# Second mixer's seven-product gates: the third product's tiles split later, forms of x in fewer steps, the norm's bias added by accumulating DMAs

## The chip, the core and the metric

One core of one Trainium2 chip runs the whole program. The metric is the device time in microseconds (us). Five engines work side by side, each on its own queue in order: TensorE (PE, with PEld for its weight loads), VectorE (DVE), ScalarE (ACT), GpSimd (POOL) and SyncE (SP). SP and POOL mostly issue DMAs here. Engines wait for one another through semaphores.

## What is computed

A trunk of two layers on x of 512 positions by 1024 channels in float32. Each layer has a token mixer and a ConvFFN, both with a residual and a layer norm:

```python
for i in range(DEPTH):                      # DEPTH = 2
    y = gla_mixer(h, ...) if i == 0 else gdn_mixer(h, ...)
    h = layer_norm(ALPHA * h + y, ln_g[i, 0], ln_b[i, 0])
    h = layer_norm(ALPHA * h + conv_ffn(h, ffn_w_in[i], ffn_conv_w[i], ffn_w_out[i]), ln_g[i, 1], ln_b[i, 1])

def gdn_mixer(x, w_in, conv_w, a_log, dt_bias, norm_w, w_out):
    qkv, gate, beta_lin, a_lin = split(x @ w_in)     # gate: 1024 columns
    ...
    o = rms_norm(gdn_chunked(qc, kc, vc, beta, gc), norm_w)
    return (from_head_chunks(o) * silu(gate)) @ w_out
```

The change is in the second mixer, the gated DeltaNet (gdn): in its projection to `gate`, 512 x 1024 by 1024 x 1024, and in the layer norm's bias that is brought back for the residual behind it.

## The kernel before, in words

**Products in split parts.** A float32 matrix product is made of three products of high and low parts (wh·xh, wl·xh, wh·xl). `split_out` (L718) makes the parts of a tile: a cast on ACT (the high part) and a subtraction on DVE (the low part). A weight tile of 128 x 1024 thus costs a load, a cast and a split.

**The gate in seven products.** `gated` (L1255 on) makes the gate's 2 x 2 block product with seven products instead of eight, in the order of `GATED` (L33): b21, b11, t1, b22, t2, t3, t4. Each is 24 "fold" matmuls, and uses two weight tiles and one *form* of x. Of the weights only b21, b11 and b22 are split as they are loaded; the others are sums, which the memory side makes: `issue_gated` (L452 to L469) splits a tile and then has POOL issue an accumulating DMA (L465) that adds the next block of the weights to the same tile. So t1's tiles (called gw) are b11's tiles with b12 added, and each is there one DMA after b11's own split. The tiles of b22 (called raw) get b12 added in the same way.

**How far ahead tiles are split.** `prefetch` (L471) issues the splits of the next tiles of the plan, as far as `self.look` says: with 3, three tiles beyond those taken. `gated` sets 3 at its start, and 2 within t3, so t4 runs with 2 in both mixers that call it.

**The order.** The program is written as coroutines that a small scheduler (`spawn`, `pump`, a model clock) puts between the matmuls when the program is built. The order in which it reaches an instruction is the order in each engine's queue; nothing is reordered at run time. A number behind `yield` tells how long the model clock waits.

**What runs beside the gate products.** While PE does the folds, the recurrence of the gdn runs in the gaps. `inverses` makes triangular inverses, the V and R matmuls of 64 x 64, in turns; DVE copies their results to the tiles `rm` (L1863 for quarters, L1883 for halves), two heads at a time. `chain(g)` (L1935 on) then walks through the four chunks of heads 0 to 3 (g = 0) and of heads 4 to 7 (g = 1): ks, vn, kT, qs, s and o on PE; on ACT `vn` (L1960) and `kd` (L1967), scaled copies out of PSUM; on DVE `yy`, the state (L1980 for the first chunk, a copy; L1983 later) and `v` (L1989, L1991). vn reads rm of all four heads; s needs vn and kd; the state copy frees a PSUM tile for later use.

**Forms of x.** `x_forms_within` makes the forms w1, v4, v2 and v3 from quarters a, b, c, d of x. a and b are sums xh + xl on DVE (L1163). c and d come through DMAs (`whole`, L1218 to L1224): first a copy of xh into a tile xq, then an accumulating DMA of xl onto it, all from POOL's queue. `both` (L1176) makes sums and differences of them, and `put` splits the result back into xh and xl.

**The residual.** The residual h lies in HBM during the mixer. `unspill` (L971) brings its eight tiles back, multiplies each by the layer norm's gain row (L989) and adds its bias row (L990) on DVE; `out_proj` (L615) then adds the mixer's output.

Of the kernel before, what the change touches and what calls it, by code (L numbers as in the profile page):

```python
# [8 lines left out]
F32 = mybir.dt.float32  # L9
# [4 lines left out]
ALU = mybir.AluOpType  # L14

P = 128
D = 1024
S = 512
# [55 lines left out]
def blk(i, n=P):  # L74
    return slice(i * n, i * n + n)


class Trunk:
# [893 lines left out]
    def unspill(self, gb_rows):  # L972

        nc = self.nc
        self.h = [[None, None] for _ in range(NTB)]
        gb = [self.slot("gb") for _ in range(4)]
        for hf in range(2):
            for tb in range(NTB):
                t = self.resid("h")
                nc.gpsimd.dma_start(t, self.hd[blk(tb), blk(hf, S)])  # L980
                self.h[tb][hf] = t
            for i in range(2):
                nc.gpsimd.dma_start(gb[2 * i + hf], gb_rows[i][blk(hf, S)].partition_broadcast(P))

        def affine():
            for hf in range(2):
                for tb in range(NTB):
                    t = self.h[tb][hf]
                    nc.vector.tensor_mul(t, t, gb[hf])  # L989
                    nc.vector.tensor_add(t, t, gb[2 + hf])  # L990
                    self.set(("h", tb, hf))
                    yield 1.8

        self.spawn(affine(), 9.0)

# [212 lines left out]
    def x_forms_within(self, forms, part, pair, full, both):  # L1208


        nc = self.nc

        def put(name, ts, odd, tok):
            for k, t in enumerate(ts):
                self.split_out(part(self.xh, odd, tok, k), part(self.xl, odd, tok, k), pair(t))
            forms[name] = (odd, tok)
            self.set(("form", name), 2.0)

        def whole(odd, tok):
            ts = [self.slot("xq") for _ in range(2)]  # L1220
            for x, op in ((self.xh, ALU.bypass), (self.xl, ALU.add)):
                for k, t in enumerate(ts):
                    nc.gpsimd.dma_start(pair(t), part(x, odd, tok, k).bitcast(F32), accum_op=op)
            return ts  # L1224

        yield from self.until(("rm", 1))
        a = full(0, 256)
        yield 1.5
        b = full(1, 256)
        yield 1.5  # L1230
        both(a, b, ALU.subtract, b)
        yield 2.0
        put("w1", b, 0, 256)
        yield from self.until(("rm", 5))
        c = whole(0, 0)
        d = whole(1, 0)
        yield from self.until(("used", "a11"))
        yield 4.0
        both(c, a, ALU.subtract, a)
        yield 2.0  # L1240
        both(b, c, ALU.subtract, b)
        yield 2.0
        both(b, d, ALU.add, d)
        c = None
        yield 2.0
        put("v4", d, 1, 0)
        d = None
        yield 3.0
        put("v2", b, 0, 0)
        b = None  # L1250
        yield from self.until(("used", "w1"))
        yield 1.0
        put("v3", a, 0, 256)

    def gated(self, forms, tag, done, last):  # L1255


        nc = self.nc
        acc = [[self.psum("fold") for _ in range(2)] for _ in range(2)]
        top, high, right = ([None, None] for _ in range(3))  # L1260

        def operand(form, c, r):
            if isinstance(forms.get(form), tuple):
                odd, tok = forms[form]
                chunk, tok = 2 * c + odd, tok + r * P
                return self.xh[:, chunk, tok:tok + P], self.xl[:, chunk, tok:tok + P]
            if form in forms:
                cols = slice(c % 2 * 256 + r * P, c % 2 * 256 + r * P + P)
                return tuple(t[:, cols] for t in forms[form][c // 2])
            chunk = 2 * c + (form != "a11")  # L1270
            tok = r * P + (256 if form == "a22" else 0)
            return self.xh[:, chunk, tok:tok + P], self.xl[:, chunk, tok:tok + P]

        def copied(ps):
            t = self.slot(tag)
            nc.scalar.copy(t, ps)
            return t

        def update(name, r):
            p, x = acc[0][r], acc[1][r]  # L1280
            if name == "b21":
                top[r] = copied(x)
            elif name == "b11":
                nc.vector.tensor_add(top[r], top[r], p)
                done(r, 1, top[r], top[r])
            elif name == "t1":
                high[r] = copied(x)
            elif name == "b22":
                right[r] = copied(x)
            elif name == "t2":  # L1290
                nc.vector.tensor_sub(right[r], right[r], p)
                done(r, 0, right[r], right[r])
            elif name == "t3":
                self.third = nc.vector.tensor_sub(high[r], high[r], p)
                self.after = None, self.third
                done(2 + r, 0, high[r], high[r])
            elif name == "t4":
                done(2 + r, 1, self.slot(tag), p)

        self.look = 3  # L1300
        for name, form, at in GATED:
            if form[0] in "vw":
                self.wait(("form", form))
            def terms(i, w, r):
                for j in range(2):
                    begin = name in ("b11", "b21", "t1") and i + j == 0
                    self.tm_terms(acc[at][r], *operand(form, i + j, r), *w[j], begin, i + j == 3, True)
                if i:
                    update(name, r)

            if name in ("t1", "t2", "t3"):
                w = [self.weight() for _ in range(2)]
                for r in range(2):
                    for i in (0, 2):
                        if name == "t3" and r and i:
                            self.look = 2
                        terms(i, w[i // 2], r)
                        if name != "t3" or not r:
                            self.pump()
                        if r:  # L1320
                            self.spend()
            else:
                for i in (0, 2):
                    w = self.weight()
                    if name == "t4":
                        self.after = ()
                    for r in range(2):
                        terms(i, w, r)
                        self.pump()
                    self.spend()  # L1330
            self.set(("used", form))
            if last:
                forms.pop(form, None)
        self.look = LOOKAHEAD
# [299 lines left out]
    def gdn(self, li, g, b):  # L1634
        nc = self.nc
# [11 lines left out]
        q, k, v, am, rm, pj = ([None] * DH for _ in range(6))  # L1647
# [284 lines left out]
        sg = [[None, None] for _ in range(NTB)]  # L1932
# [111 lines left out]
                self.spawn(finish(hf, half))  # L2044
        forms = {"apart": False}
        self.spawn(self.x_forms(forms))
        self.gated(forms, "sg", gate_done, True)
        self.wait(("r2", 1))
        self.unspill(spilled)
        self.mixer_out(y, li, g, b)  # L2050
# [76 lines left out]
```

## Time and profile before

| what | value |
|---|---|
| three runs | 1225.78, 1225.42, 1224.86 us; median 1225.42 us |
| the profiled execution | 1226.22 us, of which the span from first to last instruction is 1224.4 us |
| mean granted clock of TensorE | 0.997 |
| TensorE busy | 1212.0 us, 99% |
| VectorE, ScalarE, GpSimd busy | 75%, 51%, 15% |
| DMA traffic | 154.65 MB, mean 126 GB/s |
| the second mixer's gate products | 724 to 816 us of the span |
| the residual and the norm behind the mixer | about 820 to 855 us |

In the rows of the timeline the columns are start and length in us, engine, line of the kernel, operation, output tiles <- input tiles, shapes, and how many instructions of one kind the row joins. A bracket tells for how long the engine was idle before the row, and what ended that. In the rows of the waits stand the total, the number and the longest. Tile names are those of the program without their numbers. "DMA to landing" is the time from a DMA's issue until its data is there.

### The profile page before, as it was taken

The page shows a single profiled execution, that of the slowest core. Times are in us where ns is not written, and L with a number is a line of the kernel's source. Part 1 is how long each engine was busy: PE and PEld are TensorE (multiplying, and loading weights), DVE is VectorE, ACT ScalarE, POOL GpSimd, SP SyncE. Part 2 cuts the span into 40 slices and gives each one's busy share as a digit, 9 for nine tenths or more (in the row PEclk, how much of TensorE's full clock was granted, in tenths as well). Part 3 has the DMA queues.
Part 4 walks back from the last instruction along what each step waited for, and adds up shares of the span by engine and source line. Part 5 has one row for each costly group of instructions (what it writes and reads, how often), then busy time and mean ns, then how long its engine had stood idle before and what let it go on. Part 6 is the DMA issues. An engine that isn't in the chain of part 4 may idle for free.

```text
span 1224.4 us, 17226 instructions
## 1 busy us (share of the span) xinstructions
PE 1212.0 (99%) x6477; PEld 1023.0 (84%) x6477; DVE 923.6 (75%) x1523; ACT 628.6 (51%) x1116; POOL 179.5 (15%) x219
## 2 busy tenths in 40 slices
PE   9999999999999999999999998999999999999998
PEld 8888888988888888889888887987988888888886
DVE  6989787787767775766789966798697756775667
ACT  5666664544434443554677655873644434443440
POOL 3031101601100110001342044200520100020000
PEclk9999999999999999999999998999999999999999
DMA  8484652536733544423435259445443853393321
GB/s 233 113 165 112 135 157 67 189 104 137 196 113 104 121 93 129 128 82 105 127 108 145 82 127 155 107 149 146 131 137 97 170 180 90 99 188 89 108 65 69
DMA packets 179315, 154.65 MB, mean 126 GB/s; under 512 B 17094, under 2 KB 142090, under 8 KB 179232
## 3 DMA queue, kind: packets, MB, share of 16 engines
q1 hardware_dynamic: 161920, 115.23, 31.9%
q0 software_dynamic: 16352, 37.67, 16.1%
q8 instruction: 51, 0.84, 0.3%
q10 hardware_dynamic: 960, 0.66, 0.2%
q14 instruction: 32, 0.26, 0.1%
HBM read 133.06 MB, written 5.78 MB: 113 GB/s over the span
## 4 chain that ended last, share of the span: by engine, by line
PE 94%; DMA 2%; DVE 2%; ACT 1%; issue 0%; SPq 0%; DVEq 0%; POOL 0%; ACTq 0%; POOLq 0%
PE fm L214 54%; PE fold L214 21%; PE tm L214 11%; PE o L214 1%; PE xT L232 1%; DMA gw<-in_gdn_w_in_dram 1%; DVE wl L718 1%; PE pg L214 1%; PE yT L232 1%; DMA raw<-in_ffn_w_in_dram 0%; DMA xq<-xl 0%; PE ds L214 0%; PE V L214 0%; DMA xq<-xh 0%; PE warm L800 0%
## 5 line engine op out<-in xcount | busy, mean ns | idle before, releaser
L214 PE MATMUL fm<-xh,wh 128*128 128x512 f32 (+2 forms) x1096 | 400.4, 368 | 0.7 <-ACT xh L718 0.7
L214 PE MATMUL fm<-xl,wh 128*128 128x512 f32 (+2 forms) x1096 | 398.6, 366 | 0.0
L214 PE MATMUL fm<-xh,wl 128*128 128x512 f32 (+1 forms) x1072 | 391.4, 367 | 0.0
L718 DVE TENSOR_TENSOR wl<-raw,wh 128x1024 fp32r<-128x1024 f32 (+1 forms) x156 | 195.2, 1253 | 140.7 <-ACT wh L718 140.6
L718 ACT CAST wh<-raw 128x1024 fp32r<-128x1024 f32 (+1 forms) x157 | 162.5, 1036 | 205.6 <-PE fm L214 129.9
L214 PEld LDWEIGHTS fm<-xh,wh 128*128 128x128 f32 (+1 forms) x1096 | 205.4, 188 | 34.0 <-ACT xh L718 0.9
L214 PEld LDWEIGHTS fm<-xl,wh 128*128 128x128 f32 (+1 forms) x1096 | 205.4, 188 | 33.2 <-DVE xl L915 0.2
L214 PEld LDWEIGHTS fm<-xh,wl 128*128 128x128 f32 x1072 | 201.2, 189 | 33.1
L1021 DVE SCALAR_TENSOR_TENSOR conv<-fm,ffn_cw,conv 128x511 f32<-128x511 f32 x112 | 83.5, 746 | 9.7 <-ACT conv L1019 7.8
L718 ACT CAST wh<-b 128x1024 fp32r<-128x1024 f32 x48 | 50.2, 1053 | 74.0 <-PE fold L214 34.0
L214 PE MATMUL fold<-wh,fh 128*128 128x512 f32 x224 | 87.6, 391 | 0.0
L214 PE MATMUL fold<-wl,fh 128*128 128x512 f32 x224 | 87.3, 390 | 0.0
L214 PE MATMUL fold<-wh,fl 128*128 128x512 f32 x224 | 87.2, 389 | 0.0
L718 DVE TENSOR_TENSOR wl<-b,wh 128x1024 fp32r<-128x1024 f32 x48 | 58.4, 1223 | 22.4 <-ACT wh L718 22.0
L413 POOL DMA_DIRECT2D b<-b x24 | 20.8, 914 | 354.6 <-DVE wl L718 217.6
L1039 ACT ACTIVATE conv<-conv 128x512 f32<-128x512 f32 x44 | 27.7, 630 | 66.0 <-DVE conv L1021 66.0
L1629 DVE SCALAR_TENSOR_TENSOR conv<-fm,gdn_cw,conv 128x511 f32<-128x511 f32 (+2 forms) x72 | 54.1, 789 | 8.1 <-ACT conv L1627 7.5
L214 PEld LDWEIGHTS fold<-wh,fh 128*128 128x128 f32 x224 | 42.0, 188 | 9.7 <-DVE h L1110 1.0
L214 PEld LDWEIGHTS fold<-wh,fl 128*128 128x128 f32 x224 | 42.1, 188 | 8.8
L214 PEld LDWEIGHTS fold<-wl,fh 128*128 128x128 f32 x224 | 42.1, 188 | 8.7
L1021 DVE SCALAR_TENSOR_TENSOR form<-fm,ffn_cw,form 128x511 f32<-128x511 f32 x64 | 47.7, 746 | 1.1
L931 POOL TENSOR_TENSOR h<-h,gb 128x512 f32<-128x512 f32 x16 | 24.9, 1575 | 135.7 <-PE xT L232 134.3
(364 smaller groups left out, 2070.5 us busy)
## 6 DMA issues: line engine op xcount, KB each, us to landing
raw<-in_ffn_w_in_dram SPq DMA_DIRECT2D x88, 512.0 KB, 3.9
raw<-in_gdn_w_in_dram SPq DMA_DIRECT2D x28, 512.0 KB, 4.1
b<-in_ffn_w_out_dram SPq DMA_DIRECT2D x24, 512.0 KB, 5.9
b<-b POOLq DMA_DIRECT2D x24, 512.0 KB, 4.7
raw<-in_ffn_w_out_dram SPq DMA_DIRECT2D x20, 512.0 KB, 3.7
raw<-in_gla_w_in_dram SPq DMA_DIRECT2D x18, 512.0 KB, 4.1
gw<-in_gla_w_in_dram POOLq DMA_DIRECT2D x8, 512.0 KB, 7.1
raw<-in_gla_w_out_dram SPq DMA_DIRECT2D x8, 512.0 KB, 3.6
```

What stands on the lines that cost most here:

```text
L214: t = self.nc.tensor.matmul(out, a, b, start=start, stop=stop, skip_group_check=joined)
L232: t = self.nc.tensor.transpose(out, a, self.ident[:n, :n])
L413: self.nc.gpsimd.dma_start(out, group[src, i][:, cols], accum_op=ALU.add)
L718: return self.nc.scalar.copy(dst_h, src), self.nc.vector.tensor_sub(dst_l, src, dst_h)
L931: nc.gpsimd.tensor_mul(h[hf], h[hf], gb[hf])
L1021: nc.vector.scalar_tensor_tensor(a[:, d:], ps[:, :S - d], tap(2 - d), a[:, d:], ALU.mult, ALU.add)
L1039: nc.scalar.activation(a, a, AF.Gelu)
L1629: self.conv = nc.vector.scalar_tensor_tensor(a[:, d:], ps[:, :S - d], tap(3 - d), a[:, d:], ALU.mult, ALU.add)
```

## The change

Three edits:

1. `gated` takes a tuple `spare`. For the products named in it `look` is 1, and 2 from the last piece of b11 on; for the others it is 3. The gdn passes ("b21", "b11"). Since `look` is now set ahead of every product, t4 has 3 where it had 2, in both mixers.
2. `whole` issues the copies of xh from SP's queue and the accumulates of xl from POOL's. The forms are made in another order: b - c, b + d and v4 first, then c - a, and with fewer waits of the model clock.
3. `unspill` loads only the gain row. The bias row is added by eight DMAs of 256 KB, which read the row from HBM for all 128 partitions and accumulate onto h; the tile counts as there 6 us later in the model clock.

```diff
@@ unspill
-        gb = [self.slot("gb") for _ in range(4)]
+        gb = [self.slot("gb") for _ in range(2)]
...
-            for i in range(2):
-                nc.gpsimd.dma_start(gb[2 * i + hf], gb_rows[i][blk(hf, S)].partition_broadcast(P))
+            nc.gpsimd.dma_start(gb[hf], gb_rows[0][blk(hf, S)].partition_broadcast(P))
...
                     nc.vector.tensor_mul(t, t, gb[hf])
-                    nc.vector.tensor_add(t, t, gb[2 + hf])
-                    self.set(("h", tb, hf))
-                    yield 1.8
+                    nc.gpsimd.dma_start(t, gb_rows[1][blk(hf, S)].partition_broadcast(P), accum_op=ALU.add)
+                    self.set(("h", tb, hf), 6.0)
+                    yield 1.2
@@ x_forms_within
-            for x, op in ((self.xh, ALU.bypass), (self.xl, ALU.add)):
+            for x, queue, op in ((self.xh, nc.sync, ALU.bypass), (self.xl, nc.gpsimd, ALU.add)):
                 for k, t in enumerate(ts):
-                    nc.gpsimd.dma_start(pair(t), part(x, odd, tok, k).bitcast(F32), accum_op=op)
+                    queue.dma_start(pair(t), part(x, odd, tok, k).bitcast(F32), accum_op=op)
...
-        yield 4.0
+        yield 5.0
+        both(b, c, ALU.subtract, b)
+        both(b, d, ALU.add, d)
+        put("v4", d, 1, 0)
+        yield 3.0
         both(c, a, ALU.subtract, a)
-        yield 2.0
-        both(b, c, ALU.subtract, b)
-        yield 2.0
-        both(b, d, ALU.add, d)
-        c = None
-        yield 2.0
-        put("v4", d, 1, 0)
-        d = None
-        yield 3.0
+        c = d = None
         put("v2", b, 0, 0)
@@ gated
-    def gated(self, forms, tag, done, last):
+    def gated(self, forms, tag, done, last, spare=()):
...
-        self.look = 3
         for name, form, at in GATED:
+            self.look = 1 if name in spare else 3
...
+                    if i and name == "b11" and spare:
+                        self.look = 2
                     self.spend()
@@ gdn
-        self.gated(forms, "sg", gate_done, True)
+        self.gated(forms, "sg", gate_done, True, ("b21", "b11"))
```

The matmuls are the same in number. DVE has eight instructions fewer. Three places of the new order matter below.

**DVE, while t1's tiles are split.** Before: `wl<-gw` is the low part of a gw tile, the first two such rows here are t1's two tiles; `rm_6253` and `rm_6255` at L1883 belong to heads 2 and 3.

```order
L718 TENSOR_TENSOR wl_6752<-gw_6459,wh_6751 128x1024
L1863 COPY rm_6381<-R_6766 32x4x32
L1863 COPY rm_6383<-R_6766 32x4x32
L1907 TENSOR_SCALAR gd_x_6809<-gd_ssq_4886 128x32
L718 TENSOR_TENSOR wl_6825<-gw_6471,wh_6824 128x1024
L1163 TENSOR_TENSOR xq_6798<-xh,xl 128x512
L732 TENSOR_SCALAR gd_rr_4887<-gd_x_6809 128x32
L1883 COPY rm_6253<-R_6838 64x4x64
L733 TENSOR_SCALAR gd_rr_4887<-gd_rr_4887 128x32
L734 TENSOR_SCALAR gd_x_6809<-gd_x_6809 128x32
L1883 COPY rm_6255<-R_6838 64x4x64
```

Now, in the same queue (lines of the new program; L1880 is what L1883 was):

```order
L718 TENSOR_TENSOR wl_6899<-gw_6459,wh_6898 128x1024
L1162 TENSOR_TENSOR xq_6786<-xh,xl 128x512
L736 TENSOR_TENSOR rs_t_1060_6799<-gd_rr_4887,gd_x_6797 128x32
L1880 COPY rm_6253<-R_6824 64x4x64
L737 TENSOR_TENSOR rs_t_1060_6799<-rs_t_1060_6799,gd_rr_4887 128x32
L1880 COPY rm_6255<-R_6824 64x4x64
L738 SCALAR_TENSOR_TENSOR gd_rr_4887<-rs_t_1060_6799,gd_rr_4887 128x32
L1175 TENSOR_TENSOR xq_6786<-xq_6738,xq_6786 128x512
L736 TENSOR_TENSOR rs_t_1060_6799<-gd_rr_4887,gd_x_6797 128x32
L718 TENSOR_TENSOR xl<-xq_6785,xh 128x2x256
L737 TENSOR_TENSOR rs_t_1060_6799<-rs_t_1060_6799,gd_rr_4887 128x32
L718 TENSOR_TENSOR wl_6992<-gw_6471,wh_6991 128x1024
```

The first of t1's splits stands ahead of the rm copies in both; the second (of gw_6471) has moved behind them.

**DVE, at the first chunk of the second chain.** `xq<-xq,xq` are the sums and differences of the forms, `state<-s` is that chain's first state. Before:

```order
L1176 TENSOR_TENSOR xq_6747<-xq_6952,xq_6747 128x512
L1176 TENSOR_TENSOR xq_6797<-xq_6797,xq_6952 128x512
L1176 TENSOR_TENSOR xq_6748<-xq_6953,xq_6748 128x512
L1176 TENSOR_TENSOR xq_6798<-xq_6798,xq_6953 128x512
L1176 TENSOR_TENSOR xq_6958<-xq_6797,xq_6958 128x512
L1980 COPY state_6982<-s_7043 128x512
L1989 COPY v_6010<-o_7049 128x512
L1176 TENSOR_TENSOR xq_6959<-xq_6798,xq_6959 128x512
```

Now:

```order
L1175 TENSOR_TENSOR xq_6785<-xq_6785,xq_6940 128x512
L1175 TENSOR_TENSOR xq_6737<-xq_6940,xq_6737 128x512
L1175 TENSOR_TENSOR xq_6786<-xq_6786,xq_6941 128x512
L1175 TENSOR_TENSOR xq_6946<-xq_6785,xq_6946 128x512
L1175 TENSOR_TENSOR xq_6947<-xq_6786,xq_6947 128x512
L1175 TENSOR_TENSOR xq_6738<-xq_6941,xq_6738 128x512
L718 TENSOR_TENSOR xl<-xq_6785,xh 128x2x256
L1977 COPY state_6970<-s_7043 128x512
L1986 COPY v_6010<-o_7049 128x512
```

The tiles that come through DMAs are xq_6952, 6953, 6958 and 6959 before, and xq_6940, 6941, 6946 and 6947 now. The sum on the last of them, and a split, have moved ahead of the state copy.

**ACT, at the same place.** Before:

```order
L1960 ACTIVATE vn_6988<-vn_6983,gd_bp_4883 128x128 x4
L1967 ACTIVATE kd_6994<-kT_6993,gd_ebl_4880 128x128 x4
L1960 ACTIVATE vn_7019<-vn_7014,gd_bp_4883 128x128 x4
L1973 ACTIVATE v_5797<-qs_7034,gd_eb_4878 128x128
L1967 ACTIVATE kd_7025<-kT_7024,gd_ebl_4880 128x128 x4
```

Now:

```order
L1957 ACTIVATE vn_6976<-vn_6971,gd_bp_4883 128x128 x4
L718 CAST xh<-xq_6785 128x2x256
L1964 ACTIVATE kd_6982<-kT_6981,gd_ebl_4880 128x128 x4
L1957 ACTIVATE vn_7019<-vn_7014,gd_bp_4883 128x128 x4
L1970 ACTIVATE v_5797<-qs_7034,gd_eb_4878 128x128
L1964 ACTIVATE kd_7025<-kT_7024,gd_ebl_4880 128x128 x4
```

A cast of the form v2's first tile, xq_6785, has moved ahead of the second chain's kd.

## Prediction

> **What bounds the kernel now.** I read the first part of the page, then the waits of TensorE, then what stands around the longest of them on each engine.
>
> ```profile
> PE 1212.0 (99%) x6477; PEld 1023.0 (84%) x6477; DVE 923.6 (75%) x1523; ACT 628.6 (51%) x1116; POOL 179.5 (15%) x219
> ```
> ```profile
> PE vn L214 <- DVE rm L1883: 4.7, 1, 4.7
> PE warm L800 <- POOL one L103: 1.0, 1, 1.0
> PE xT L232 <- DVE ln_rs L878: 0.8, 1, 0.8
> ```
>
> TensorE is busy for 1212.0 of 1224.4 us. The diff takes nothing from its work, so the change can win only what TensorE waits, and what its half clock costs. The one long wait is 4.7 us at the chain's vn in the second mixer. Its place, first on PE, then on DVE:
>
> ```profile
> 739.64 0.60 PE L214 MATMUL vn<-v,rm 128*128 128x128 f32 x4
> 744.91 0.80 PE L214 MATMUL vn<-v,rm 128*128 128x128 f32 x2 [4.66 <-DVE rm L1883]
> ```
> ```profile
> 738.89 1.23 DVE L718 TENSOR_TENSOR wl<-gw,wh 128x1024 fp32r<-128x1024 f32 x1 [3.07 <-ACT wh L718]
> ...
> 742.62 1.23 DVE L718 TENSOR_TENSOR wl<-gw,wh 128x1024 fp32r<-128x1024 f32 x1 [1.91 <-ACT wh L718]
> ```
>
> Heads 2 and 3 of vn need the rm copies of the second head group. Those are short (0.33 us in the chain below), but stand in DVE's queue behind both splits of the third product, t1. A split waits for its cast, the cast for the accumulating DMA that makes t1's tile out of b11's. The chain of waits says so step by step, and the windows show what follows:
>
> ```profile
> 732.75 8.71 DMA gw<-in_gdn_w_in_dram
> 741.54 1.05 ACT wh L718
> 742.62 1.23 DVE wl L718
> 743.84 0.60 DVE xq L1163
> 744.54 0.33 DVE rm L1883
> ...
> 748.89 2.26 PE fold L214 x6
> ...
> 784.18 1.38 PE fold L214 x6
> ```
> ```profile
> 740.25:743.40 3.15, 0.00 (x0) 0.00 (x0) 1.24 (x4) 1.81 (x3) 1.18 (x1) 1.00 0.39 33
> 743.50:746.90 3.40, 1.99 (x8) 1.68 (x8) 3.40 (x13) 1.71 (x4) 1.19 (x1) 0.50 1.05 149
> 746.90:750.20 3.30, 3.30 (x36) 2.94 (x36) 2.18 (x7) 2.96 (x10) 1.90 (x3) 0.50 0.83 137
> ```
>
> Columns are the window, its length, busy time of PE, PEld, DVE, ACT and POOL, then granted clock, DMA share and GB/s. After the gap the clock stands at 0.50 for two windows, 6.7 us. Six fold matmuls (the last two rows of the chain) then took 2.26 us, against 1.38 later. TensorE was busy for 1.99 + 3.30 = 5.29 us in the slow windows; slowed like the folds that is 2.1 us lost, if everything is halved 2.6. I take 2.4, as small matmuls fill most of it. The place costs 4.66 + 2.4 = 7.1 us. The Trainium skill (TensorE: Matmul & The Clock Gate, "What's actually happening") says that the gate falls to half after one idle window of 3413 ns, free-running. These rows agree: 4.66 us idle, then 0.50.
>
> **The change part by part.** *Later splits.* With the smaller look, the first split of b11 moves behind the two rm copies of the first group and an xq sum, the second also behind two dt products. From the durations of these rows (0.35 to 0.65 us each in DVE's queue) b11's splits end near 732.1 and 734.7, where before the accumulate behind the second could issue at 732.75. In the new order only t1's *second* split has moved behind the second group's rm copies; the first still stands ahead. So a wait stays. How long it is hangs on the landing of t1's first tile:
>
> ```profile
> DMA to landing us min/median/max: 6.3/6.6/8.7
> ```
>
> This is the gw tile's row between 731 and 744.5 us. Issued at about 732.45 and landing after the median 6.6, the tile is there at 739.0. Cast 1.05, split 1.23, then an xq sum (0.6), a short rs_t step and two rm copies put vn's heads 2 and 3 at about 742.5, 2.25 us after the four matmuls that end at 740.24. The 8.7 is the second of two that were under way together, and now some 2.6 us lie between their issues, so I take the median; the ends give 742.2 to 744.6. With 2.25 us of gap I take the clock as staying at 1.00, which the first window still shows 3.15 us into the gap. Gain here: 4.66 - 2.25 = 2.4, and 2.4 for the clock.
>
> *Forms of x.* The plain copies xq<-xh go from POOL's queue to SP's, and the steps on DVE come in another order. Before:
>
> ```profile
> 756.39 4.91 POOL L1223 DMA_DIRECT2D xq<-xl  x4 [2.15 <-DMA xq<-xh]
> ```
> ```profile
> DMA to landing us min/median/max: 3.8/5.9/6.9
> ```
> ```profile
> 723.11 77.00 SPq L327 DMA_DIRECT2D raw<-in_gdn_w_out_dram  x3
> ```
> ```profile
> 760.21 1.29 DVE L1176 TENSOR_TENSOR xq<-xq,xq 128x512 f32<-128x512 f32 x2 [1.27 <-DMA xq<-xl]
> ...
> 763.52 0.69 DVE L1176 TENSOR_TENSOR xq<-xq,xq 128x512 f32<-128x512 f32 x1 [0.40 <-DMA xq<-xl]
> 764.13 0.68 DVE L1980 COPY state<-s 128x512 f32<-128x512 f32 x1
> ...
> 765.33 0.68 DVE L1176 TENSOR_TENSOR xq<-xq,xq 128x512 f32<-128x512 f32 x1
> ```
> ```profile
> 761.32 1.16 PE L214 MATMUL s<-vn,kd 128*128 128x128 f32 x8
> ...
> 766.00 1.06 PE L214 MATMUL o<-vn,dt 128*128 128x128 f32 x8
> ```
> ```profile
> 760.13 1.14 ACT L1967 ACTIVATE kd<-kT,gd_ebl 128x128 f32<-128x128 f32 x4 [1.52 <-PE vn L214]
> ```
> ```profile
> 758.00:764.50 6.50, 6.24 (x46) 5.61 (x45) 4.51 (x9) 4.44 (x18) 4.53 (x4) 1.00 1.10 162
> ```
>
> Four accumulates of xl are issued from 756.39 on, after 2.15 us of waiting for the copies they add to. The first has landed when DVE's sum can start at 760.2 (X1), the third by 763.5, and the fourth (X4), another step of 1.6 us on, near 765, since the sum on it starts at 765.33 without a wait. They stay on POOL in the same order, behind the accumulate of a raw tile. What gets earlier is their start: the copies of xh go out as soon as their tiles are free, at some 744 to 750, on SP, which issues nothing else between 723 and about 800 but three loads of output weights (the row says so; those behind the copies are not needed before), and POOL has nothing else before xl from about 749. So I put X1 at 756.3 (753 to 758) and X4 at 760.9 (756.5 to 762). The first bound is an issue at 749 and the 3.8 us that a forms' DMA took at best (second row); the DMA share of 1.10 says that the engines are full there, and keeps me from taking it.
>
> Two waits come with the new order. On ACT, a cast xh<-xq now stands ahead of the second chain's kd; it waits for a DVE sum, and that for X1. With 0.65 for the sum, 0.6 for a cast of half the width of the chain's 1.05, and 1.1 for the four of kd, kd is done at 756.3 + 2.3 = 758.6. TensorE without any further wait would want it at 761.32 - 4.8 + 0.4 for a fold piece that now stands ahead of s, about 756.9. Behind it in ACT's queue stand vn, v and kd of the other head group. On DVE, all six sums and an xl split now stand ahead of the state copy, where before the sum that needs X4 stood behind it. The copy is done four steps of 0.6 us after X4, at 763.4, and the second o (766.00 before) waits for the PSUM tile that this copy frees. Without the two waits that o would start at 766.00 - 2.4 - 2.4 = 761.2. So of 4.8 us about 2.6 come through (X4 at 762: 1.5; early: all 4.8). Break-even at this place is X4 = 763.6. Behind that o the order of TensorE has fold groups moved between the chain's steps, and ACT has one cast fewer ahead of its vn, so I put nothing there (0 to 0.5 lost).
>
> The Trainium skill (DMA: Bandwidth & Descriptors, "Issuing engines are not separate DMA queues") speaks against a gain from the move to SP, since the same 16 engines do the work; by it alone the xl landings would stay where they were, which is the last rival below. The DMA share of 1.10 agrees with it.
>
> *Bias by DMA.* Eight adds leave DVE:
>
> ```profile
> L990 DVE TENSOR_TENSOR h<-h,gb x8: 684/697/698, 826.1 to 846.9; 128x512 f32<-128x512 f32 x8
> ```
> ```profile
> 820.00:830.00 10.00, 10.00 (x53) 8.47 (x52) 10.00 (x19) 6.91 (x11) 0.00 (x0) 1.00 0.25 79
> ```
> ```profile
> 835.88 0.69 DVE L615 SCALAR_TENSOR_TENSOR h<-h,tm 128x512 f32<-128x512 f32 x1
> ```
> ```profile
> 844.10 5.61 DMA raw<-in_ffn_w_in_dram
> ```
>
> DVE is full there and starts a step every 0.6 us, so 4.8 us come free. The layer norm behind it shows 0.8 us of wait (xT on ln_rs); its chain goes back through a weight load that could only start at 844.10, when a DVE split had freed the tile. With six of the adds gone ahead of that split it starts over 3 us earlier, and the 0.8 go. Two loads of the bias on POOL go as well; nothing waited for them. What could take their place: the eight accumulates, 256 KB each on POOL, idle in this stretch (0.00) with a DMA share of 0.25. Issued from about 825.6 to 831 at some 1.2 us each, and landing within 8.7 at worst, the first is there by 834.3, ahead of the first residual step at 835.88. Next late is nothing that the waits show. If the cover were gone, one landing too late by d costs d.
>
> The first mixer's last product also keeps a look of 3; a few splits change places under full cover: nothing, within 0.5 us.
>
> Sum: -2.6 - 0.8 = -3.4 us on the profiled run's own 1226.22 us (1.8 of it lies outside the span): 1222.8. That run is 0.8 above the median of 1225.42, so about **1222.0 us**.
>
> **The rivals.** *Clean removal.* If the forms' tiles land early (X4 by 758.7), neither new wait is late: 4.8 + 0.8, or 1225.42 - 5.6 = 1219.8. The minimum of 3.8 in the forms' row speaks for it, the full DMA engines against.
>
> *It does not do what it says.* t1's first split still stands ahead of the rm copies. If its tile again takes 8.7 us, vn starts at 744.6, the gap is 4.4, the clock halves, and only 0.3 at vn and 0.8 at the norm are won: 1224.3. The same lies behind a second way: if kd and the state copy come late enough to make one gap of 3 us, the half clock's 2.4 come back, and 1225.42 - 3.4 + 2.4 = 1224.4.
>
> *Slower: the state copy behind all of xl.* If the accumulates land as late as before (X1 760.2, X4 765, what full engines or a copy held up on SP would do), kd is done at 762.5, TensorE idles 5.6 us at s, the half clock moves here with its 2.4, and the second o starts at 765 + 2.4 = 767.4, 1.4 later than now. In all 1.4 + 2.4 - 0.8 = 3.0 more: 1228.4. With the norm's 0.8 it is slower from X4 = 764.4 on, or from some 762 when the clock falls as well. The share of 1.10 speaks for it; that POOL has 3 us less to issue ahead of the xl speaks against it.
>
> **How the numbers follow.** Forecast (a gain of 2.5 to 5) 0.50, clean removal 0.13, half-removed 0.24, slower 0.13. The likeliest is 1222.0. The range goes from just below clean removal, 1219.5, up through the half-removed cases to 1226.5, and leaves out most of the slower rival and what is won beyond clean removal. A measurement tells 0.2%, or 2.45 us: faster is below 1222.97, slower above 1227.87. The forecast lies just beyond the first; of its 0.50 I count 0.42 as faster, with clean removal 0.55. Of the slower rival 0.10 passes the bound. The rest, 0.35, is the same within the bound.
>
> **What would show it.** In the trace of the changed kernel: vn's wait on rm near 2.2 us instead of 4.66, a granted clock of 1.00 after it, then a wait of about 1.7 us at s on ACT's kd and one at the second o on the state copy; no wait at xT on ln_rs; no line of adds in the affine. I am wrong if vn still waits over 3 us or the clock falls; if xl lands before 758 (then more is won), or after 763.6 (then it is slower); or if the residual step waits for a bias DMA.

## The result, and the profile after

The changed kernel takes 1235.28 us (median of 4, 1233.0 to 1236.33), against 1225.6 before: 9.7 us slower, a ratio of 1.0075 (95% interval 1.0062 to 1.0089). Its profiled execution took 1235.68 us with a span of 1233.7, 9.3 above the span before. The forecast was 1222.0, with a range to 1226.5. TensorE's longest waits now:

```profile
PE xT L232 <- DVE h L894: 4.4, 1, 4.4
PE s L214 <- ACT kd L1964: 4.1, 1, 4.1
PE vn L214 <- DVE rm L1880: 3.4, 1, 3.4
```

One long wait has become three. Where the time came from is seen by laying the same steps of TensorE side by side:

| step on TensorE | before | after | shift |
|---|---|---|---|
| first vn, first part | 739.64 | 739.93 | +0.3 |
| first vn, last part starts | 744.91 | 743.89 | -1.0 |
| qs of the first chain, second chunk | 760.36 | 758.68 | -1.7 |
| the second o | 766.00 | 769.66 | +3.7 |
| the mixer's output product ends | 853.7 | 857.4 | +3.7 |
| first xT behind the norm | 854.44 | 861.76 | +7.3 |
| end of the span | 1224.4 | 1233.7 | +9.3 |

So the gain at vn is there: 1.0 us at vn's last part, 1.7 us by 760. It is lost again within the next 10 us, and a second loss of 5.6 us lies at the norm. The first place, on PE and in windows (columns as in the prediction):

```profile
743.89 1.23 PE L214 MATMUL vn<-v,rm 128*128 128x128 f32 x4 [3.36 <-DVE rm L1880]
```
```profile
764.12 1.47 PE L214 MATMUL s<-vn,kd 128*128 128x128 f32 x8 [4.14 <-ACT kd L1964]
765.38 1.92 PE L214 MATMUL o<-vn,dt 128*128 128x128 f32 x8
```
```profile
743.90:745.90 2.00, 2.00 (x8) 1.53 (x8) 2.00 (x8) 1.90 (x5) 0.27 (x1) 0.61 0.53 45
745.90:747.90 2.00, 2.00 (x34) 1.88 (x33) 1.12 (x2) 1.44 (x6) 0.69 (x1) 0.54 0.95 159
759.97:764.10 4.13, 0.00 (x1) 0.00 (x0) 1.99 (x3) 1.70 (x6) 2.61 (x3) 1.00 0.87 134
764.15:765.50 1.35, 1.35 (x9) 1.35 (x10) 0.69 (x1) 1.21 (x5) 0.33 (x1) 0.75 1.01 153
765.50:767.00 1.50, 1.50 (x10) 1.50 (x9) 1.14 (x2) 1.32 (x6) 0.00 (x0) 0.50 1.02 87
```

After the 3.36 us the clock falls as before (0.61 and 0.54 over 4 us, which is 3.4 us at one half, instead of 6.8 before); after the new gap at s it falls again (0.75, 0.50). What s waits for is read back through ACT, DVE, POOL and SP:

```profile
762.40 0.62 ACT L718 CAST xh<-xq 128x512 fp32r<-128x512 f32 x1 [5.47 <-DVE xq L1175]
762.93 1.14 ACT L1964 ACTIVATE kd<-kT,gd_ebl 128x128 f32<-128x128 f32 x4
```
```profile
761.67 2.10 DVE L1175 TENSOR_TENSOR xq<-xq,xq 128x512 f32<-128x512 f32 x3 [4.50 <-DMA xq<-xl]
764.48 0.69 DVE L1175 TENSOR_TENSOR xq<-xq,xq 128x512 f32<-128x512 f32 x1 [0.70 <-DMA xq<-xl]
765.86 1.29 DVE L1175 TENSOR_TENSOR xq<-xq,xq 128x512 f32<-128x512 f32 x2 [0.69 <-DMA xq<-xl]
767.07 0.68 DVE L718 TENSOR_TENSOR xl<-xq,xh 128x512 fp32r<-128x512 f32 x1
767.67 0.69 DVE L1977 COPY state<-s 128x512 f32<-128x512 f32 x1
```
```profile
750.33 1.18 POOL L465 DMA_DIRECT2D raw<-in_gdn_w_in_dram  x1 [1.93 <-DVE gd_rr L738]
756.38 2.41 POOL L1222 DMA_DIRECT2D xq<-xl  x2 [4.87 <-DMA xq<-xh]
```
```profile
747.95 4.50 SPq L1222 DMA_DIRECT2D xq<-xh  x4
```

The cast ahead of kd waits 5.47 us for a sum that waits for the first xl landing, X1, at 761.7 (760.2 before). The copies of xh go out on SP from 747.95, and POOL can still start on xl only at 756.38; before, with the copies on POOL, it was 756.39. The first copy is issued 1.2 us earlier than before (749.19), and the copies take longer to land: 8.5 us at the median, 6.7 before. So the move between the queues brought nothing forward.

At the norm, on ACT, then DVE, the bias DMAs' landing time, and windows of the place:

```profile
833.78 1.14 ACT L718 CAST wsh<-raw 128x512 fp32r<-128x512 f32 x2 [3.20 <-DMA raw<-in_gdn_w_out_dram]
843.10 1.14 ACT L718 CAST wsh<-raw 128x512 fp32r<-128x512 f32 x2 [8.18 <-DMA raw<-in_gdn_w_out_dram]
849.74 1.05 ACT L718 CAST wh<-raw 128x1024 fp32r<-128x1024 f32 x1 [5.50 <-DMA raw<-in_ffn_w_in_dram]
```
```profile
843.75 1.29 DVE L718 TENSOR_TENSOR wsl<-raw,wsh 128x512 fp32r<-128x512 f32 x2 [5.86 <-ACT wsh L718]
844.96 0.68 DVE L615 SCALAR_TENSOR_TENSOR h<-h,tm 128x512 f32<-128x512 f32 x1
```
```profile
DMA to landing us min/median/max: 5.4/10.0/12.4
```
```profile
830.00:834.00 4.00, 4.00 (x19) 3.26 (x18) 4.00 (x8) 0.80 (x2) 3.53 (x5) 1.00 0.70 173
834.00:838.00 4.00, 4.00 (x19) 3.24 (x18) 3.89 (x7) 0.92 (x2) 3.42 (x4) 1.00 1.07 175
838.00:842.00 4.00, 4.00 (x19) 3.22 (x18) 0.00 (x0) 0.00 (x0) 0.00 (x0) 1.00 1.05 208
842.00:846.00 4.00, 4.00 (x19) 3.30 (x18) 2.22 (x4) 1.14 (x2) 0.00 (x0) 1.00 1.12 212
857.40:861.70 4.30, 0.00 (x0) 0.00 (x0) 3.92 (x11) 0.80 (x2) 0.00 (x0) 0.85 1.02 286
861.80:863.40 1.60, 1.60 (x9) 1.60 (x9) 1.47 (x4) 0.39 (x2) 0.00 (x0) 0.50 1.13 325
```

The same stretch before, from 834 to 846:

```profile
834.00:838.00 4.00, 4.00 (x19) 3.21 (x19) 3.98 (x8) 1.57 (x2) 0.00 (x0) 1.00 0.35 103
838.00:842.00 4.00, 4.00 (x19) 3.24 (x18) 3.69 (x7) 0.90 (x1) 0.00 (x0) 1.00 0.45 131
842.00:846.00 4.00, 4.00 (x19) 3.34 (x18) 4.00 (x6) 0.67 (x2) 0.00 (x0) 1.00 0.25 67
```

And the landing, in us at the end of the row, of the last load of output weights and of the first FFN load behind it, before (issued at 829.27 and 832.27) and now (833.1 and 836.71):

```profile
raw<-in_gdn_w_out_dram SPq DMA_DIRECT2D x1, 512.0 KB, 3.7
raw<-in_ffn_w_in_dram SPq DMA_DIRECT2D x1, 512.0 KB, 3.7
```
```profile
raw<-in_gdn_w_out_dram SPq DMA_DIRECT2D x1, 512.0 KB, 10.0
raw<-in_ffn_w_in_dram SPq DMA_DIRECT2D x1, 512.0 KB, 12.9
```

The DMA share is above 1.0 from 834 on, where it was 0.25 to 0.45 before. A load of output weights lands after 10.0 us instead of 3.7, and ACT's cast of it waits 8.18 us; its splits stand on DVE ahead of the first residual step (L615), and hold it until 844.96 (835.88 before, where the kernel was 3.7 us earlier). DVE and ACT are idle from 838 to 842, and the late FFN load holds them again (the cast at 849.74 waits 5.50 us). The norm's xT then waits 4.4 us, and the clock is at 0.50 behind that.

### The profile page after: what moved, and what is told of

Its sections match the earlier page's. It is cut to its first block, busy times and chain, and to the rows that moved or that the text cites. A ratio compares the mean times of both kernels' runs of the same rounds, so it can differ in the third digit from the quotient of the medians.

```text
span 1233.7 us, 17255 instructions
## 1 busy us (share of the span) xinstructions
PE 1215.2 (99%) x6477; PEld 1025.5 (83%) x6477; DVE 917.9 (74%) x1515; ACT 629.0 (51%) x1116; POOL 181.1 (15%) x221
## 4 chain that ended last, share of the span: by engine, by line
PE 83%; DVE 7%; DMA 4%; ACT 2%; issue 2%; SPq 1%; POOL 0%; DVEq 0%; ACTq 0%; POOLq 0%
PE fm L214 47%; PE fold L214 20%; PE tm L214 10%; DVE conv L1626 2%; PE o L214 2%; DVE wl L718 1%; PE xT L232 1%; DMA gw<-in_gdn_w_in_dram 1%; DMA raw<-in_ffn_w_in_dram 1%; ACT dt L1690 1%; DVE tmp L1786 1%; DVE tt L1788 1%; DMA xq<-xh 1%; ACT wh L718 0%; PE ds L214 0%
## 5 line engine op out<-in xcount | busy, mean ns | idle before, releaser
L214 PE MATMUL fold<-wh,xh 128*128 128x512 f32 x104 | 43.5, 418 | 0.2
```

Of the source, the lines that this page charges most:

```text
L214: t = self.nc.tensor.matmul(out, a, b, start=start, stop=stop, skip_group_check=joined)
```

## The experiments

Two theories were to be told apart. *A*: two separate losses, one in the chain and one made by the bias DMAs at the norm. *B*: one loss, the late chain that pushes the norm's loads. Within A it was open whether the chain's loss comes from the order of the queues (A1) or from the later landing of the forms' tiles (A2, then X). Each median stands beside the kernel before on the same chip.

**no_bias**: the change without its third edit (the two loads of the bias row come back too; these lines leave them out).

```diff
-                    nc.gpsimd.dma_start(t, gb_rows[1][blk(hf, S)].partition_broadcast(P), accum_op=ALU.add)
-                    self.set(("h", tb, hf), 6.0)
-                    yield 1.2
+                    nc.vector.tensor_add(t, t, gb[2 + hf])
+                    self.set(("h", tb, hf))
+                    yield 1.8
```

> The change without its third edit: the bias is added on DVE as before; the splits and the forms are as in the changed kernel. Theory A (two separate losses: the second chain's kd and state stand behind sums that wait for the xl DMAs, and the bias DMAs slow the weight loads at the norm): the chain's loss stays, 4.1 us at s and a half clock, and the norm's wait falls from 4.4 back to about 0.8; about 3.4 us slower than before, some 1229. Theory B (one loss: the late chain pushes the norm's loads, the bias DMAs cost nothing): still about 9 us slower, 1234 to 1235.

Measured: 1229.3 us against 1225.81, ratio 1.0028 (1.0018 to 1.0039). At the norm xT no longer waits, but the wait at s is still there:

```profile
PE s L214 <- ACT kd L1965: 3.8, 1, 3.8
```

**bias_only**: before, with the third edit (the diff of no_bias the other way round).

> Before, with the third edit alone. Theory A: the norm's wait of 4.4 us and the half clock behind it come with this edit alone; 5 to 6 us slower than before, about 1231. Theory B: the norm's wait of 0.8 us goes and nothing takes its place; 0 to 0.8 us faster, about 1225.

Measured: 1230.94 against 1225.81, ratio 1.0040 (1.0025 to 1.0055).

```profile
PE xT L232 <- DVE h L894: 4.1, 1, 4.1
```

Theory A holds, and B falls: 3.5 and 5.1 us, 8.6 of the 9.7 together. The bias DMAs make the norm's wait with no late chain ahead of it.

**look_only**: before, with the first edit (`spare` and `look`, as in the diff above).

> Before, with the first edit alone (later splits); the forms are made in the old order and by POOL, and kd stands ahead of the cast of a form. Theory A1 (the order of ACT's and DVE's queues makes the loss in the chain): no wait at s; vn waits about 3.4 us; the second o is bounded by the state copy behind the third xl landing as before, so 0 to 2 us faster than before, about 1224.5. Theory A2 (the later splits push every later accumulate, so the chain is late in any order): the second o is as late as in the changed kernel, about 3.4 us slower, 1229.

Measured: 1226.91 against 1225.81, ratio 1.0010 (1.0000 to 1.0020): 1.1 slower, where A1 said up to 2 faster and A2 3.4 slower. Its ten runs spread from 1225.7 to 1228.7 us and the profiled one took 1226.1, so the 1.1 is not to be read closely. vn waits 3.2 us, and kd, now ahead of the casts, is in time. But on ACT, the next vn is not:

```profile
762.80 1.14 ACT L1962 ACTIVATE vn<-vn,gd_bp 128x128 f32<-128x128 f32 x4 [2.74 <-DVE xq L1176]
```

This is the first chain's second chunk. In the built program its tile takes the memory of c's first tile, so it waits for the last sum that reads c, which waits for X1. The first o behind it starts at 764.00, 2.6 us after X1 at 761.4; before it started at 762.73, 2.5 after X1 at 760.2. So X1 was the wall before the change too, and the old wait at vn had hidden it. bias_none below, whose chain is that of the kernel before, shows the same: there vn's half clock happened to be shorter and the first chain's s came 1.6 us earlier (749.40 for 750.98), but the first o then waited 1.6 us for ACT's vn and started at 762.48.

**look_sp**: look_only, with the xh copies on SP.

```diff
-            for x, op in ((self.xh, ALU.bypass), (self.xl, ALU.add)):
+            for x, queue, op in ((self.xh, nc.sync, ALU.bypass), (self.xl, nc.gpsimd, ALU.add)):
                 for k, t in enumerate(ts):
-                    nc.gpsimd.dma_start(...)
+                    queue.dma_start(...)
```

> As look_only, with the copies of xh from SP as well; the forms are made in the old order, but the sum on the last xl tile stands ahead of the state copy. If SP's queue brings the xl landings forward (the forecast: X4 near 761), about 2 to 3 us faster than before, 1223. If the landings stay where they were (X1 about 761, X4 about 765), no wait at s, since kd is ahead of the cast, and the second o waits for the state copy until about 767: 0 to 2 us slower, about 1226.5.

Measured: 1227.89 against 1225.81, ratio 1.0016 (1.0007 to 1.0026). X1 is at 761.2, within 0.3 of look_only. The wait stands at the first o:

```profile
763.73 0.80 PE L214 MATMUL o<-vn,dt 128*128 128x128 f32 x2 [3.83 <-ACT vn L1962]
```

The time is 2.1 us above before; the landings stayed, as the second case said, but the wait stands at the first o and not at the second. With kd ahead of the cast the wait is as long (3.8) as with kd behind it in no_bias (3.8). In look_only, look_sp and no_bias X1 is the same within 0.3 us (761.4, 761.2 and 761.2), and the first step of TensorE that is held by it starts 2.4 to 2.6 us later. The order decides which step that is and what is left to do behind it: the wait is 2.5, 3.8 and 3.8 us, the clock falls to one half behind the last two alone, and the second o starts at 767.05, 768.58 and 769.29. So of the chain's 3.5 us the later splits alone make 1.1, the copies from SP, with the order that the program then gets, 1.0 more, and the forms' new order the last 1.4; these are differences of medians, each good to about 1 us.

**look_dve**: look_only, with c and d as sums on DVE.

```diff
-        c = whole(0, 0)
-        d = whole(1, 0)
+        c = full(0, 0)
+        yield 1.5
+        d = full(1, 0)
+        yield 1.5
```

> As look_only, but the quarters c and d of x are sums on DVE instead of eight DMAs. Theory X (the xl landings are the wall in the chain, before the change as well as after: besides the sums that need them, the tile of vn for the next chunk is c's memory): no wait at s or o; vn waits about 3.2 us as in look_only; about 3 to 4 us faster than before, 1222. Theory Y (something else in the chain, such as ACT's or DVE's load, bounds it): the four sums add 2.4 us to DVE, and the time stays at 1225 to 1228.

Measured: 1222.58 against 1225.99, ratio 0.9971 (0.9959 to 0.9983). No wait at s or o is left, vn waits 3.3 us. Theory X holds: without the eight DMAs the wall is gone. The 3.4 us are those of both edits; dve_forms tells what the sums on DVE make alone, 1.6, so 1.8 are left for the later splits.

**dve_forms**: before, with the same edit.

> Before, with c and d as sums on DVE and nothing else changed. Theory X: the wait at vn stays at 4.7 us with its half clock; behind it there was only 0.26 us of wait for the forms, so 0 to 0.5 us faster. If the DMAs of the forms slowed the accumulates of the weights beside them, up to 1.5 us faster. Theory Y: slower by up to 2.4 us, the four sums.

Measured: 1224.38 against 1225.99, ratio 0.9987 (0.9977 to 0.9996); vn waits 4.8 us. The 1.6 us are at the upper end of what was expected, and what makes them was not followed further.

**bias_quarter** and **bias_plain**: bias_only with the DMA's size or kind changed, the queues the same.

```diff
-  nc.gpsimd.dma_start(t, gb_rows[1][blk(hf, S)].partition_broadcast(P), accum_op=ALU.add)
+  nc.gpsimd.dma_start(t[:, :P], gb_rows[1][hf * S:hf * S + P].partition_broadcast(P), accum_op=ALU.add)  # quarter
+  nc.gpsimd.dma_start(t, gb_rows[1][blk(hf, S)].partition_broadcast(P))                                  # plain
```

> As bias_only, with the same instructions in the same order, but each bias DMA adds only 128 of its 512 columns, so a quarter of the bytes (the rest of the bias is left out). Theory T (the bytes that the eight DMAs move fill the DMA engines and hold the weight loads up): the norm's wait falls from 4.1 us to under 1, time 1225 to 1226.5. Theory Q (what costs is the new order on DVE and POOL, or a fixed cost of each DMA): it stays near 4 us and 1231.

> As bias_only, same instructions in the same order and the same bytes, but the eight DMAs overwrite h instead of adding to it (so the residual is left out). If bytes alone count, the weight loads are as late: wait about 4 us, 1231. If it is the adding that is slow in the DMA engines, the wait falls under 1.5 us, 1225 to 1227.

Measured: 1228.3 and 1228.68 against 1225.99, ratios 1.0020 (1.0010 to 1.0029) and 1.0026 (1.0016 to 1.0035); xT waits 1.8 and 2.7 us. Neither expectation was met: a quarter of the bytes leaves about half of the loss in time, and so does the full size without adding. The software queue's share of the DMA engines from 822 to 852, with packets and MB, in bias_only, bias_plain and bias_quarter:

```profile
q0 software_dynamic: 1152, 2.10, 41.9%
```
```profile
q0 software_dynamic: 640, 2.10, 31.1%
```
```profile
q0 software_dynamic: 1152, 0.52, 14.9%
```

**bias_none**: bias_only, without the eight DMAs.

```diff
-                    nc.gpsimd.dma_start(t, gb_rows[1][blk(hf, S)].partition_broadcast(P), accum_op=ALU.add)
```

> As bias_only, every queue in the same order, but without the eight bias DMAs (the norm's bias is left out). Theory T (the DMAs hold up the weight loads): without them the loads land in 4 to 5 us, the wait at the norm is at most 0.8, time 1224 to 1225.5. Theory Q (the new order on DVE, the residual steps behind the weight splits, costs by itself): a wait of 1 us or more stays, 1227 to 1229.

Measured: 1224.73 against 1226.18, ratio 0.9990 (0.9981 to 0.9999). The wait of xT on DVE is gone, and the first residual step is where it was:

```profile
835.65 0.69 DVE L615 SCALAR_TENSOR_TENSOR h<-h,tm 128x512 f32<-128x512 f32 x1 [1.20 <-PE tm L214]
```

So the queues' order costs nothing by itself, and taking the adds from DVE, with two loads of the bias row, is worth 1.5 us (0.1 to 2.3). What costs is the eight DMAs beside the weight loads. In the profiled executions the load of output weights that is issued beside them (828.4 to 829.1), and the time that TensorE takes from the second o to the first xT behind the norm, went like this:

| run | landing of the load, us | second o to first xT, us | clock behind xT |
|---|---|---|---|
| bias_none | 3.7 | 87.52 | 1.00 |
| bias_quarter | 8.0 | 89.46 | 1.00 |
| bias_plain | 8.4 | 90.34 | 1.00 |
| bias_only | 10.3 | 91.87 | 0.50 |

Up to xT plain writing makes 2.8 of the 4.3 us, and the adding the other 1.5. Behind xT only bias_only, with the longest gap, has the half clock as well. A quarter of the bytes still makes 1.9; that fits the packets, which are as many as in bias_only, but no run varies their number alone.

**force_dve**: look_dve, and t1's splits held behind the rm copies of heads 2 and 3. Issuing them later in the program alone does not move the first one in DVE's queue: the builder also orders an engine's instructions by its own estimate, so the section on the kernel is too simple where it says that the order in which the program reaches an instruction is the order in the queue. So an order edge is added.

```diff
+                    if i and name == "b11" and spare:
+                        self.look = 0
                     w = self.weight()
...
+        low = self.split_out(wh, wl, t)[1]
+        if name == "t1" and group["spare"]:
+            self.behind(low, self.rm_copy)      # the copy into rm of head 3
```

> As look_dve, and both of the third product's splits are held behind the rm copies of heads 2 and 3 on DVE, which the change did for the second split alone. If vn's wait of 3.3 us is that one split's place in the queue: vn waits nothing, a wait of 1 to 2 us may show behind it where V and R wait for ACT, the clock stays full, and the time is 2 to 4 us below look_dve, about 1219.5. If the tile's landing is needed there anyway: the wait moves to the third product's first matmul, and the time is that of look_dve, 1222.5.

Measured: 1219.41 against 1226.18, ratio 0.9945 (0.9929 to 0.9962). vn runs without a pause; V waits 1.9 us behind it for ACT, at a full clock:

```profile
739.45 1.05 PE L214 MATMUL vn<-v,rm 128*128 128x128 f32 x8
```
```profile
742.83 0.27 PE L214 MATMUL V<-T,am 64*64 64x64 f32 x1 [1.90 <-ACT V L1888]
```

This is faster than both kernels, by 6.8 us than before, where look_dve is 3.4 faster: holding the first split as well is worth the other 3.4.

**force_early_dve**: force_dve, with b11 split as early as before.

```diff
-            self.look = 1 if name in spare else 3
+            self.look = {"b21": 2, "b11": 1}[name] if name in spare else 3
```

> As force_dve, but b11's tiles are split as early as before the change, so the accumulates for the third product start earlier. If the landing of the third product's tiles is what is late next, 1 to 2 us below force_dve; if ACT's or DVE's load is, the same as force_dve.

Measured: 1221.7 against 1226.18, ratio 0.9964 (0.9953 to 0.9976), slower than force_dve, which was not expected. vn waits 2.6 us for rm again; why the copies come later here was not followed.

## Why the prediction was wrong, point by point

**vn's wait.** The mechanism was right: t1's first split still stood ahead of the rm copies. The size was off: its tile was issued at 732.82, not 732.45, and cast 7.6 us later, not 6.6, so the wait was 3.36 us, not 2.25, and the clock fell after all.

```profile
732.82 1.25 POOL L465 DMA_DIRECT2D gw<-in_gdn_w_in_dram  x1 [15.60 <-DVE wl L718]
740.38 1.04 ACT L718 CAST wh<-gw 128x1024 fp32r<-128x1024 f32 x1 [5.48 <-DMA gw<-in_gdn_w_in_dram]
```

Nor was a full clock sure at 2.25 us: the last section shows that a gap of 2.60 us can halve it. force_dve shows, without the forms' DMAs, what the edit would have been worth if it had moved both splits.

**The step that failed in the chain** is "What gets earlier is their start", with X1 at 756.3 and X4 at 760.9. X1 came at 761.7, X4 near 765.8. The copies went out at 747.95 rather than from 744, since SP waited for an R matmul until then, and landed after 8.5 us instead of 6.7, so that the first xl could start no earlier than before. Beside them the accumulates of the weights were 2 to 3 us later than before (742.99, 747.21 and 750.33 for 740.41, 744.14 and 748.30); that these made the copies slower fits the DMA share of about 1, but no run takes it apart. With the later splits alone (look_only) X1 was already 1.2 us late. The Trainium skill's sentence that was set against the edit (DMA: Bandwidth & Descriptors, "Issuing engines are not separate DMA queues") agrees with the runs: look_sp moved X1 by 0.3 us. A second step failed with it: "Without the two waits that o would start at 766.00 - 2.4 - 2.4 = 761.2". Before the change that chain was already held by X1; the 0.26 us that the first o waited for ACT's vn was its only trace, since the wait at vn had put TensorE just as late. look_only and look_sp show that with kd ahead of the cast there is still a wait for X1, at another step, though the order changes what it costs (1.1, 2.1 and, in no_bias, 3.5 us); look_dve takes it away, and its second o starts at 763.92.

The last rival described this place: X1 and X4 as late as before, kd behind the cast, the half clock at s. It put the second o at 767.4 plus 2.4 for the clock, 3.8 later than now; measured 3.7. It had 0.13. That the numbers meet so well is partly luck: X1 came 1.5 us later than it assumed, the gap at s was 4.1 us and not 5.6, and the second o did not wait for the state copy (done at 768.36) but for TensorE, which was busy without a pause from 764.12 until it started at 769.66.

**The bias.** "Next late is nothing that the waits show" failed. The sum had priced the DMAs' own landing against the first step that reads them, and not what they do to the weight loads queued at the same engines. The share of 0.25 that it read was that of 820 to 830; the DMAs were issued from 830.36 and landed after 10.0 us at the median (8.7 at worst by the sum), so they lay on the loads of 830 to 846. There the share went from 0.25 to 0.45 up to 1.05 to 1.12, a load landed after 10.0 us instead of 3.7, and the splits of that load, ahead of the residual steps in DVE's queue, passed the delay on. Forecast -0.8, measured +5.1 alone. The half that was right is that the adds on DVE cost something: 0.8 by the forecast, and 1.5 us come back in bias_none, where nothing replaces them.

By parts, then: the chain -2.6 forecast and +3.5 measured, the norm -0.8 and +5.1. The 1.1 us that the two parts leave of the whole is no larger than the intervals allow, and was not traced.

## What to carry to other kernels

A long wait hides whatever would have been late at the same time: before a wait is priced as gain, look behind it for steps with almost no slack (here a wait of 0.26 us), and follow what they wait for. A DMA that replaces a cheap instruction can be paid for by the transfers beside it; price it by the DMA share of the stretch in which it will land and by which loads are due there, not by its own landing alone. In a queue in order, moving an instruction moves the wait, and can change what it costs by a us or two, but the wait went here only when the transfer behind it did.

## What the runs showed of the hardware that was not expected

**A gap of 2.60 us halved the clock, and another of 2.66 us did not.** In the clock records of these traces every stretch of half clock behind a gap lasts 3.41 or 6.83 us, and all changes of one trace lie whole multiples of 3.41 us apart. So the time can be cut into pieces of 3.41 us at these points. First force_early_dve, where vn waits 2.60 us, then bias_plain, where xT waits 2.66 (the number behind POOL's is the granted clock):

```profile
737.55:740.97 3.42, 2.74 (x34) 2.21 (x30) 1.71 (x8) 1.99 (x3) 0.00 (x0) 1.00 0.81 135
740.97:744.38 3.41, 1.49 (x14) 1.19 (x16) 3.38 (x12) 2.70 (x5) 0.00 (x0) 1.00 0.00 1
744.38:747.79 3.41, 3.41 (x36) 2.94 (x33) 2.93 (x7) 3.35 (x10) 2.05 (x2) 0.50 0.07 6
```
```profile
849.18:852.59 3.41, 3.41 (x17) 2.83 (x16) 3.41 (x5) 1.05 (x1) 0.00 (x0) 1.00 0.38 112
852.59:856.00 3.41, 1.50 (x7) 0.92 (x5) 3.03 (x9) 0.29 (x1) 0.00 (x0) 1.00 1.02 288
856.00:859.41 3.41, 2.66 (x16) 2.40 (x17) 3.03 (x11) 1.14 (x3) 0.00 (x0) 1.00 0.98 294
```

The first gap lies so that one piece holds 1.92 us without a matmul (3.41 less the 1.49 of PE); the next piece, though full of work, has 0.50. The second is shared by two pieces, the emptier of which holds 1.91, and the clock stays. In the thirteen traces, over all gaps of a microsecond or more between 730 and 870, a piece with 2.2 us idle or more was followed by half a clock every time, one with 1.91 or less never; of two with 1.92 one was (the other is in bias_quarter). Full clock came back behind a piece with next to no idle time (at most 0.04 us), and not behind one with 1.0 or more. By these numbers a gap between about 2 and 4 us, an estimate since TensorE's ends are modelled, can halve the clock or not by where it falls. The Trainium skill (TensorE: Matmul & The Clock Gate, "What's actually happening") asks for one idle window of 3413 ns, free-running: the length agrees with the 3.41 us here, but the window need not be idle throughout.

**In these runs adding took more of the DMA engines' time than writing, and small pieces more than their bytes.** From the three queue rows above, over 30 us: 2.10 MB took 12.6 us of all engines when added, in 1152 packets, and 9.3 when written, in 640; 0.52 MB added in pieces a quarter as long, again in 1152 packets, took 4.5 us, 8.6 us per MB against 6.0. A packet's time may hold some waiting for others: the same 3.15 MB of loads beside them took 11.7 us in bias_only and 10.4 in bias_plain.
